# A gated network's first and last tiles in halves, and split weights whose rests are made by adding transfers

## The chip, the cores and the metric

The kernel runs as one program on one core of a Trainium2 chip. The metric is the device time of a run in microseconds (us). The kernel before has a median of 1264.14 us over 3 runs (1260.24 to 1267.88). One further execution was recorded by the hardware profiler; rows of that record are what this document quotes. Engines are named as the profile names them: PE is TensorE (PEld its weight loads), DVE is VectorE, ACT is ScalarE, POOL is GpSimd, SP is SyncE, whose queue starts most transfers. "L257" is line 257 of the kernel before.

## The reference, cut to what matters

The program is a decoder trunk of two layers on x of 512 tokens by 1024 features, fp32. Layer 0 mixes tokens with a state-space block, layer 1 with a forgetting attention (FoX). Behind each mixer stands a gated network:

```python
def conv_ffn(h, w_up, conv_w, conv_b, w_down):
    up = h @ w_up                       # 1024 -> 2 * 2816
    a, b = jnp.split(up, 2, axis=-1)
    ap = jnp.pad(a, ((0, 0), (CONV_W - 1, 0), (0, 0)))
    a_conv = conv_b
    for i in range(CONV_W):             # CONV_W = 3, causal, per feature
        a_conv = a_conv + ap[:, i:i + S] * conv_w[i]
    return (jax.nn.silu(a_conv) * b) @ w_down   # 2816 -> 1024
```

Ahead of every block x is normalised by its root mean square and modulated by shift and scale; the block's result is gated and added to x. At the end stands one more root-mean-square norm. The change is in the second gated network, which is the last block, and in that final norm.

## The kernel before, in words

**Layout.** Features lie on the partitions, tokens along the free axis: h is 8 tiles of 128 features by 512 tokens. The two halves of 256 tokens are HALVES; work is cut by them wherever a norm is in the way, because a norm needs all features of a token, not all tokens. The 2816 inner features are 22 pairs f of tiles (m = 2f goes through the convolution and silu, m = 2f + 1 multiplies it).

**Split products.** PE multiplies at reduced precision, so every operand is cut into a high part and a rest: hi is the value rounded by a copy on ScalarE (L240), lo is value − hi, a subtraction on VectorE (L241). Both are in `put_parts` (L238). A product is then three matmuls: hi·hi, hi·lo, lo·hi (`mms`, L249; its matmul is L257). A weight tile is loaded by SP into a buffer named raw (L161; ring of three), and split into w_hi and w_lo (rings of five). The raw buffer is free for the next load when both parts are made. Activations are kept as a_hi and a_lo, written by the norm (L390 makes nm_h, L393 a_hi, L394 a_lo).

**`product` (L262).** It multiplies output tiles ms one after the other. With head = n, the first n tiles are made half by half, so that PE can begin when only the first 256 tokens are normed. With tail = n the last n tiles are made half by half, all for the first half and then all for the second, so that the norm of the first half runs beside the second half's products. The first half's factors are spread to rows by four small matmuls (`rms_rows`, L370) placed ahead of the very last tile's second half; the inverse roots come from a chain of eleven small VectorE instructions (`inv_root`, L351 to L361, rs_v to rs_y).

**Second gated network (`ffn`, L513, with `plain` = 0 to 3).** The pairs f = 0 to 3 (tiles m0 to m7) are plain split products; m0 and m1 are in halves (head 2). From f = 4 on `quarters` (L466) makes a pair by a scheme with 7 instead of 8 block products, of 12 matmuls with 256 columns each (L500): the weights a (a11, a12) and b (a21, a22) are used as they are and in sums s1 to s4 made by VectorE (L472), the activations in x sums (L442, a_hi + a_lo) and four forms (L449), which `forms_x` (L432) yields step by step, so that they can be made between the tiles of f = 0 to 3. The results of block products are copied by ScalarE (L507, nm_h) and added by VectorE. Weights are split four times for a quarter: a, (s1, s2), (s4, s3), a22.

The 22 pairs stand in four groups of 6, 5, 6 and 5. While group q is made, the down product of group q − 1 is made too, one or two of its 8 tiles behind every pair; the last group's down product follows at the end, its last 2 tiles in halves. Its evacuation (L323) adds to h and squares it for the final norm.

**Final norm (`norm_out`, L400).** For the first half ScalarE scales h into hg, VectorE multiplies it by the rows (L411), SP stores it (L413, four stores). For the second half PE turns the tiles first (L419), and then ScalarE and VectorE apply rs_y (L424, L425, into o_tok), so that the chain of inv_root runs beside the turning. hg of the first half and o_tok share the room of a_lo, hg of the second half has that of a_hi.

**Order.** The order on each engine is fixed when the program is built, by a scheduler that works from the order of the code, priorities (`issue_after`, `behind`) and its own estimates; on the chip each engine then takes its instructions strictly in that order and waits by semaphores.

Of the kernel before, what the change touches and what calls it, by code (L numbers as in the profile page):

```python
# [8 lines left out]
F32 = mybir.dt.float32  # L9
F32R = mybir.dt.float32r  # L10
I32 = mybir.dt.int32
AF = mybir.ActivationFunctionType
# [26 lines left out]

GROUPS = (11, 11)  # L40
QGROUPS = (6, 5, 6, 5)
FIRST = (("c", (KT,)), ("s5_prm", (3, G // 2)), ("s5_eye", (64,)), ("s5_causal", (L,)))
REST = (
    ("ident", (P,)), ("ada_b", (4, 24)), ("norm_g", (4, KT)), ("final_g", (KT,)), ("cmask", (P,)), ("fox_bf", (NH,)),
# [10 lines left out]
class Trunk:  # L55
# [6 lines left out]
    def __init__(self, tc, io, ctx):  # L62
        self.tc, self.nc, self.io, self.ctx = tc, tc.nc, io, ctx
        nc = self.nc
        pool = lambda name, bufs, **k: ctx.enter_context(tc.tile_pool(name=name, bufs=bufs, **k))
        self.const = pool("const", 1)
        self.act = pool("act", 1)
        self.wpool = pool("wpool", 3)
        self.tmp = pool("tmp", 2)
        self.small = pool("small", 2)  # L70
        self.dram = pool("dram", 1, space=DRAM)
        self.mm = pool("mm", 4, space=PSUM)
        self.aux = pool("aux", 4, space=PSUM)
        self.bg = []
        self.acc = None
        self.pending = None

        self.first = self.load_pack("first", FIRST)
        self.c = self.first["c"]
        self.ones = self.const.tile([P, P], F32, name="ones")  # L80
        nc.vector.memset(self.ones, 1.0)
        self.sc = self.const.tile([P, KT], F32, name="sc")
        nc.scalar.activation(self.sc, self.c, AF.Silu)
        self.sc32 = self.const.tile([P, KT, 32], F32, name="sc32")

        self.sel = self.const.tile([P, 6], F32, name="sel")
        nc.gpsimd.memset(self.sel, 0.0)
        for q in range(4):
            for c in (q, 4 + q % 2):
                nc.gpsimd.memset(self.sel[32 * q:32 * q + 1, c:c + 1], 1.0)  # L90
        self.par = [self.const.tile([P, 24], F32, name=f"par{i}") for i in range(4)]
        self.ga = [self.const.tile([P, KT], F32, name=f"ga{i}") for i in range(4)]
# [139 lines left out]
    def split(self, src, shape, pool=None, bufs=WB):  # L232

        hi, lo = ((pool or self.wpool).tile(shape, F32R, name=n, bufs=bufs) for n in ("w_hi", "w_lo"))
        self.put_parts(hi, lo, self.raw(shape, src))
        return hi, lo

    def put_parts(self, hi, lo, src):  # L238
        nc = self.nc
        nc.scalar.activation(hi, src, AF.Copy)  # L240
        nc.vector.tensor_tensor(lo, src, hi.bitcast(F32), ALU.subtract)  # L241

    def weights(self, w, nk, *pool):
# [17 lines left out]
    def product(self, w, ms, nk, x, evac, head=0, tail=0, after=None, ticks=0, halves=HALVES, tail_pool=(), first=None, step=None):  # L261


        ms = list(ms)
        full = slice(0, S)
        if head:
            wk = first or {m: self.weights(w[m], nk) for m in ms[:head]}
            ps = {m: self.mm.tile([P, S], F32, name="mmp") for m in ms[:head]}
            for c in halves:
                for k in range(nk):  # L270
                    for m in ms[:head]:
                        self.mms(ps[m][:, c], wk[m], x, k, nk, c)
                    self.finish_norm((k + 1) * head)
                    if step:
                        step(3)
            for m in ms[:head]:
                evac(m, ps[m], full)
                self.tick(ticks)
        for m in ms[head:len(ms) - tail]:
            wk = self.weights(w[m], nk)  # L280
            ps = self.mm.tile([P, S], F32, name="mmp")
            for k in range(nk):
                self.mms(ps, wk, x, k, nk, full)
                if step:
                    step()
            evac(m, ps, full)
            self.tick(ticks)
        if tail:
            last = ms[len(ms) - tail:]
            wk = {m: self.weights(w[m], nk, *tail_pool) for m in last}  # L290
            for c in HALVES:
                for m in last:
                    if c is HALVES[1] and m == last[-1]:
                        rb = self.rms_rows(y)
                    ps = self.mm.tile([P, S // 2], F32, name="mmp")
                    for k in range(nk):
                        self.mms(ps, wk[m], x, k, nk, c)
                    evac(m, ps, c)
                if c is HALVES[0]:
                    y = after[0](c)  # L300
                else:
                    y2 = after[0](c)
                    after[1](HALVES[0], y, rb)
            self.pending = lambda: after[1](HALVES[1], y2)
# [95 lines left out]
    def norm_out(self, out):  # L400

        nc = self.nc

        def apply(cols, y, rb=None):
            last = cols is HALVES[1]
            hg = self.act.tile([P, KT, S // 2], F32, name="hg", tag="a_hi" if last else "a_lo")
            if not last:
                for k in range(KT):
                    nc.scalar.activation(hg[:, k], self.h[:, k, cols], AF.Copy, scale=self.final_g[:, k:k + 1])
                for k in range(KT):  # L410
                    nc.vector.tensor_tensor(hg[:, k], hg[:, k], rb, ALU.mult)  # L411
                    if k % 2:
                        nc.sync.dma_start(out[0][:, k - 1:k + 1], hg[:, k - 1:k + 1])  # L413
                return
            turned = [[pl.tile([P, S], F32, name=n) for pl, n in ((self.mm, "mmp"), (self.aux, "aux"))] for _ in range(2)]
            for k in range(KT):
                nc.scalar.activation(hg[:, k], self.h[:, k, cols], AF.Copy, scale=self.final_g[:, k:k + 1])
                for b in range(2):
                    nc.tensor.transpose(  # L419
                        turned[b][k // 4][:, k % 4 * P:(k % 4 + 1) * P], hg[:, k, b * P:(b + 1) * P], self.ident  # L420
                    )
            o = self.act.tile([P, 2, 2, S], F32, name="o_tok", tag="a_lo")
            for b in range(2):
                nc.scalar.activation(o[:, b, 0], turned[b][0], AF.Copy, scale=y[:, b:b + 1])  # L424
                nc.vector.tensor_scalar(o[:, b, 1], turned[b][1], y[:, b:b + 1], None, op0=ALU.mult)  # L425
                for j in range(2):
                    (nc.scalar if j == 0 else nc.sync).dma_start(out[1][:, b, j], o[:, b, j])

        return (self.rms_stats, apply), None


    def forms_x(self, pool, x):  # L432

        nc = self.nc
        H, N = KT // 2, S // 2
        t1, t2 = HALVES
        b = []
        for j, n in enumerate(("ghi1", "glo1")):
            t = pool.tile([P, H, S], F32, name=f"x{j}", tag=n)
            for c in HALVES:  # L440
                k = slice(j * H, (j + 1) * H)
                nc.vector.tensor_tensor(t[:, :, c], x[0][:, k, c].bitcast(F32), x[1][:, k, c].bitcast(F32), ALU.add)  # L442
                yield
            b.append(t)
        self.tx = {}
# [18 lines left out]
    def quarters(self, pool, l, f, x, finish):  # L464
# [10 lines left out]
        def parts(src, names, *where):  # L475
            hi, lo = ((where[0] if where else self.wpool).tile(
                [P, len(names) * H, P], F32R, name=n, tag=(where[1] + n if where else n), bufs=1 if where else WB
            ) for n in ("w_hi", "w_lo"))
            self.put_parts(hi, lo, src)
            for j, n in enumerate(names):  # L480
                w[n] = hi[:, j * H:(j + 1) * H], lo[:, j * H:(j + 1) * H]

# [48 lines left out]
    def ffn(self, i, l, x, nxt, ticks=0, plain=None):  # L531

        nc, tc = self.nc, self.tc
        with tc.tile_pool(name=f"ffn{l}", bufs=1, reuse_waits="tile") as pool:
# [40 lines left out]
            for q, n in enumerate(groups):  # L575
# [4 lines left out]
                        down(q, range(KT))  # L580
                    continue
                for j, f in enumerate(fs):
                    if f in plain:
                        up([f], head=0 if f else 2)
                        if f == 0:
                            todo.append(self.forms_x(pool, x))
                        for _ in range(3):
                            if todo and next(todo[0], True):
                                todo.pop()
                    else:  # L590
                        while todo:
                            if next(todo[0], True):
                                todo.pop()
                        self.quarters(pool, l, f, x, gated)
                    if q:
                        down(q - 1, range(j * KT // n, (j + 1) * KT // n))
            down(last, range(KT), tail=2, tail_pool=(pool, 4))
        return y

    def dump(self, out):  # L600
# [920 lines left out]
```

## Time and profile before

| | before |
|---|---|
| median of 3 runs | 1264.14 us (1260.24 to 1267.88) |
| the profiled execution's own time | 1263.7 us |
| its span | 1261.9 us |
| PE busy | 1235.6 us, 98% of the span |
| DVE busy | 897.0 us, 71% |
| ACT busy | 566.6 us, 45% |
| POOL busy | 56.5 us, 4% |
| DMA | 183.21 MB, mean 145 GB/s |
| mean granted PE clock | 0.994 |
| second gated network | about 893 to 1250 us |

Times in rows are microseconds from the span's start. A row of a timeline has start, duration, engine, line, operation, output <- inputs, shapes, and in square brackets how long the engine stood idle ahead of it and what ended that. "x3" puts neighbouring instructions of one kind together; durations of matmuls overlap, since they are pipelined, so the pace of PE is read from the chain of work, where pieces of PE follow each other.

### The profile page before, as it was taken

The numbers are of one execution on the slowest core, as the hardware profiler recorded it, in microseconds if no ns is written. First come the engines' busy times: TensorE is split into PE (matmuls) and PEld (weight loads), VectorE is DVE, ScalarE is ACT, GpSimd is POOL, SyncE is SP. The second block draws the span as 40 slices with busy tenths as digits, with TensorE's granted clock in tenths as the row PEclk, the third lists the DMA queues.
The fourth block names the chain that finished last, engine by engine and source line by source line (L and its number), as shares of the span: only waits on it lengthen the run. The fifth ranks groups of instructions, "written<-read, shape, count | busy, mean of one in ns | idle before, by whom it ended". The sixth has DMA issues, their size and how long they took to land.

```text
span 1261.9 us, 19246 instructions
## 1 busy us (share of the span) xinstructions
PE 1235.6 (98%) x7410; PEld 1022.5 (81%) x7410; DVE 897.0 (71%) x1606; ACT 566.6 (45%) x1041; POOL 56.5 (4%) x103
## 2 busy tenths in 40 slices
PE   7999999999999999999999999999999999999996
PEld 2566678898878778788799888878879999999985
DVE  7978887578764646656566567766899878887854
ACT  3544445335332233333433466664366555555543
POOL 0000000000000000000000233430000000000000
PEclk9999999999999999999999999999999999999998
DMA  9768667327644736544413424322043232343221
GB/s 360 242 217 257 209 197 237 102 96 240 227 149 142 227 120 229 168 151 152 149 35 117 153 99 140 126 88 68 19 134 105 90 118 82 105 129 97 91 73 67
DMA packets 73066, 183.21 MB, mean 145 GB/s; under 512 B 23079, under 2 KB 25471, under 8 KB 71951
## 3 DMA queue, kind: packets, MB, share of 16 engines
q1 hardware_dynamic: 72687, 181.46, 44.6%
q8 instruction: 58, 0.95, 0.3%
q10 hardware_dynamic: 288, 0.52, 0.1%
q14 instruction: 33, 0.27, 0.1%
HBM read 175.04 MB, written 6.92 MB: 144 GB/s over the span
## 4 chain that ended last, share of the span: by engine, by line
PE 93%; DVE 3%; ACT 1%; DMA 1%; issue 0%; SPq 0%; DVEq 0%; ACTq 0%
PE mmp L257 56%; PE mmp L500 10%; PE mmp L1102 4%; PE aux L500 4%; PE mmp L1267 2%; PE aux L908 2%; PE mmp L1131 2%; PE aux L1409 2%; PE aux L1392 1%; PE mmp L180 1%; PE aux L997 1%; PE aux L989 1%; PE aux L1362 1%; PE mmp L1042 1%; PE aux L947 1%; PE mmp L1072 1%
## 5 line engine op out<-in xcount | busy, mean ns | idle before, releaser
L240 ACT ACTIVATE w_hi<-raw 128x1024 fp32r<-128x1024 f32 (+4 forms) x201 | 186.3, 930 | 270.1 <-PE mmp L257 220.2
L241 DVE TENSOR_TENSOR w_lo<-raw,w_hi 128x1024 fp32r<-128x1024 f32 (+4 forms) x201 | 215.5, 1074 | 90.4 <-ACT w_hi L240 86.4
L257 PE MATMUL mmp<-a_hi,w_hi 128*128 128x512 f32 (+1 forms) x616 | 233.8, 382 | 3.5 <-ACT a_hi L393 2.1
L257 PE MATMUL mmp<-a_lo,w_hi 128*128 128x512 f32 (+1 forms) x616 | 231.2, 376 | 0.9 <-DVE a_lo L394 0.9
L257 PE MATMUL mmp<-a_hi,w_lo 128*128 128x512 f32 (+1 forms) x616 | 231.3, 377 | 0.0
L257 PE MATMUL mmp<-ghi,w_hi 128*128 128x512 f32 (+1 forms) x384 | 145.5, 379 | 0.0
L257 PE MATMUL mmp<-glo,w_hi 128*128 128x512 f32 (+1 forms) x384 | 145.0, 378 | 0.0
L257 PE MATMUL mmp<-ghi,w_lo 128*128 128x512 f32 (+1 forms) x384 | 145.0, 378 | 0.0
L257 PEld LDWEIGHTS mmp<-a_hi,w_hi 128*128 128x128 f32 x616 | 115.2, 188 | 28.1 <-ACT w_hi L240 3.3
L257 PEld LDWEIGHTS mmp<-a_hi,w_lo 128*128 128x128 f32 x616 | 115.8, 188 | 21.5 <-DVE w_lo L241 0.4
L257 PEld LDWEIGHTS mmp<-a_lo,w_hi 128*128 128x128 f32 x616 | 116.0, 188 | 20.9 <-DVE a_lo L394 1.3
L323 DVE SCALAR_TENSOR_TENSOR h<-mmp,par,h 128x512 f32<-128x512 f32 (+1 forms) x72 | 49.4, 689 | 65.3 <-PE mmp L257 65.1
L257 PEld LDWEIGHTS mmp<-ghi,w_lo 128*128 128x128 f32 x384 | 72.5, 189 | 14.6
L257 PEld LDWEIGHTS mmp<-ghi,w_hi 128*128 128x128 f32 x384 | 72.6, 189 | 14.0
L257 PEld LDWEIGHTS mmp<-glo,w_hi 128*128 128x128 f32 x384 | 72.5, 189 | 13.9
L208 DVE SCALAR_TENSOR_TENSOR ada_acc<-ada_raw,sc,ada_acc 128x1024 f32<-128x1024 f32 x49 | 62.8, 1281 | 29.1 <-DMA ada_raw<-in_ada_w 28.6
L500 PE MATMUL mmp<-w_hi 128*128 128x256 f32 x216 | 60.6, 280 | 0.0
L500 PE MATMUL mmp<-w_hi,w_lo 128*128 128x256 f32 x216 | 60.5, 280 | 0.0
L500 PE MATMUL mmp<-w_lo,w_hi 128*128 128x256 f32 x216 | 60.5, 280 | 0.0
L552 ACT ACTIVATE conv<-conv 128x512 f32<-128x512 f32 x44 | 27.7, 631 | 65.3 <-DVE conv L549 65.0
L1102 PE MATMUL mmp<-a_x,raw 128*128 128x512 f32 x112 | 56.5, 644 | 0.0
L241 DVE TENSOR_TENSOR w_lo<-sums,w_hi 128x1024 fp32r<-128x1024 f32 x36 | 43.8, 1220 | 4.8 <-ACT w_hi L240 4.7
(298 smaller groups left out, 2480.6 us busy)
## 6 DMA issues: line engine op xcount, KB each, us to landing
raw<-in_w_up SPq DMA_DIRECT2D x88, 512.0 KB, 3.8
ada_raw<-in_ada_w SPq DMA_DIRECT2D x56, 512.0 KB, 4.4
raw<-in_ada_w SPq DMA_DIRECT2D x40, 512.0 KB, 6.4
raw<-in_w_down SPq DMA_DIRECT2D x32, 384.0 KB, 3.1
raw<-in_w_down SPq DMA_DIRECT2D x32, 320.0 KB, 2.9
nf<-nfd SPq DMA_DIRECT2D x8, 1152.0 KB, 5.7
raw<-in_fox_qk SPq DMA_DIRECT2D x16, 512.0 KB, 3.6
h<-in_x SPq DMA_DIRECT2D x8, 512.0 KB, 5.5
```

The lines of the kernel that those rows point to most:

```text
L208: nc.vector.scalar_tensor_tensor(acc, w, self.sc[:, k:k + 1], acc, op0=ALU.mult, op1=ALU.add)
L240: nc.scalar.activation(hi, src, AF.Copy)
L241: nc.vector.tensor_tensor(lo, src, hi.bitcast(F32), ALU.subtract)
L257: self.last_mm = self.nc.tensor.matmul(o, wt, xt[:, cols], start=(k == 0 and n == 0), stop=(k == nk - 1 and n == 2),)
L323: self.nc.vector.scalar_tensor_tensor(self.h[:, m, cols], ps, self.par[i][:, 16 + m:17 + m], self.h[:, m, cols], op0=ALU.mult, op1=ALU.add,)
L500: self.last_mm = nc.tensor.matmul(o, wt[:, k], xt[:, k], start=(first and k == 0 and n == 0), stop=(k == H - 1 and n == 2), skip_group_che ...
L552: nc.scalar.activation(t, t, AF.Silu)
L908: nc.tensor.matmul(ps[g2][:, j, cols], x[rows, a + j, r].rearrange("p c j -> p (c j)"), self.rr[rows, planes, q, :], start=(j == 0 and r = ...
L1102: nc.tensor.matmul(ps, w[m][:, k, :], x[:, k], start=(k == 0), stop=(k == KT - 1))
L1131: nc.tensor.matmul(gps[m], wt, xt[:, k], start=(k == 0 and part == 0 and xt is yhi), stop=(k == KT - 1 and part == 1))
L1267: self.last_mm = nc.tensor.matmul(ps[q, b][:, :n], xt[:, k, tb], wt, start=(k == 0 and i == 0), stop=(k == KT - 1 and i == 2),)
L1409: nc.tensor.matmul(pv[:, c * P:], self.v[:, hp, k, r].rearrange("p t d -> p (t d)"), pp[:, r, c + 3 * k:NB + 3 * k, :].rearrange("p b t -> ...
```

## The change

1. m0, m1 and m2 are made in halves (head 3 over the first two pairs), m3 in full behind them. The forms are stepped four at a time instead of three.
2. The x sums of the forms are issued after the last a_lo of the norm.
3. The last network's last four down tiles are in halves instead of two; `rms_rows` of the first half stands ahead of the third of these four tiles in the second half.
4. Both halves of hg lie in one tile in a_hi's room; o_tok alone uses a_lo's.
5. `put_parts` can make the rest in another way. ScalarE copies the value a second time with sign −1 into lo, where it is rounded as hi is, and a transfer of GpSimd's queue adds raw to it, so that lo is value − hi again. It is used for a, for a22, and for the down tiles made beside pairs of groups 1 to 3 (60 splits); the sums s1 to s4, the plain tiles and the last down product keep the subtraction. Raw is free when the transfer has landed.

```diff
...
 GROUPS = (11, 11)
 QGROUPS = (6, 5, 6, 5)
+TAIL = 4
...
         self.aux = pool("aux", 4, space=PSUM)
         self.bg = []
         self.acc = None
+        self.adds = False
         self.pending = None
         self.first = self.load_pack("first", FIRST)
...
     def split(self, src, shape, pool=None, bufs=WB):
         hi, lo = ((pool or self.wpool).tile(shape, F32R, name=n, bufs=bufs) for n in ("w_hi", "w_lo"))
-        self.put_parts(hi, lo, self.raw(shape, src))
+        self.put_parts(hi, lo, self.raw(shape, src), self.adds)
         return hi, lo
-    def put_parts(self, hi, lo, src):
+    def put_parts(self, hi, lo, src, adds=False):
+
         nc = self.nc
         nc.scalar.activation(hi, src, AF.Copy)
+        if adds:
+            nc.scalar.activation(lo, src, AF.Copy, scale=-1.0)
+            nc.gpsimd.dma_start(lo, src, accum_op=ALU.add)
+            return
         nc.vector.tensor_tensor(lo, src, hi.bitcast(F32), ALU.subtract)
     def weights(self, w, nk, *pool):
...
             wk = {m: self.weights(w[m], nk, *tail_pool) for m in last}
             for c in HALVES:
                 for m in last:
-                    if c is HALVES[1] and m == last[-1]:
+                    if c is HALVES[1] and m == last[tail // 2]:
                         rb = self.rms_rows(y)
                     ps = self.mm.tile([P, S // 2], F32, name="mmp")
                     for k in range(nk):
...
     def norm_out(self, out):
         nc = self.nc
+        rooms = []
         def apply(cols, y, rb=None):
             last = cols is HALVES[1]
-            hg = self.act.tile([P, KT, S // 2], F32, name="hg", tag="a_hi" if last else "a_lo")
+            if not last:
+                rooms.append(self.act.tile([P, 2, KT, S // 2], F32, name="hg", tag="a_hi"))
+            hg = rooms[0][:, int(last)]
             if not last:
                 for k in range(KT):
                     nc.scalar.activation(hg[:, k], self.h[:, k, cols], AF.Copy, scale=self.final_g[:, k:k + 1])
...
         nc = self.nc
         H, N = KT // 2, S // 2
         t1, t2 = HALVES
+        normed = self.last_lo.ins
         b = []
         for j, n in enumerate(("ghi1", "glo1")):
             t = pool.tile([P, H, S], F32, name=f"x{j}", tag=n)
             for c in HALVES:
                 k = slice(j * H, (j + 1) * H)
-                nc.vector.tensor_tensor(t[:, :, c], x[0][:, k, c].bitcast(F32), x[1][:, k, c].bitcast(F32), ALU.add)
+                with self.tc.issue_after(normed):
+                    nc.vector.tensor_tensor(t[:, :, c], x[0][:, k, c].bitcast(F32), x[1][:, k, c].bitcast(F32), ALU.add)
                 yield
             b.append(t)
         self.tx = {}
...
             hi, lo = ((where[0] if where else self.wpool).tile(
                 [P, len(names) * H, P], F32R, name=n, tag=(where[1] + n if where else n), bufs=1 if where else WB
             ) for n in ("w_hi", "w_lo"))
-            self.put_parts(hi, lo, src)
+            self.put_parts(hi, lo, src, "s1" not in names and "s4" not in names)
             for j, n in enumerate(names):
                 w[n] = hi[:, j * H:(j + 1) * H], lo[:, j * H:(j + 1) * H]
...
                         down(q, range(KT))
                     continue
                 for j, f in enumerate(fs):
-                    if f in plain:
-                        up([f], head=0 if f else 2)
-                        if f == 0:
-                            todo.append(self.forms_x(pool, x))
-                        for _ in range(3):
+                    if f == 0:
+                        up([0, 1], head=3)
+                        todo.append(self.forms_x(pool, x))
+                    elif f in plain:
+                        if f > 1:
+                            up([f])
+                        for _ in range(4):
                             if todo and next(todo[0], True):
                                 todo.pop()
                     else:
...
                                 todo.pop()
                         self.quarters(pool, l, f, x, gated)
                     if q:
+                        self.adds = True
                         down(q - 1, range(j * KT // n, (j + 1) * KT // n))
-            down(last, range(KT), tail=2, tail_pool=(pool, 4))
+                        self.adds = False
+            down(last, range(KT), tail=TAIL if plain else 2, tail_pool=(pool, 4))
         return y
     def dump(self, out):
```

## The prediction

> **What bounds the kernel now.** First the page's head, then a table of busy time by stretch (start:end, length, then busy us and instructions of PE, PEld, DVE, ACT, POOL; granted clock; DMA share; GB/s) over the second gated network and the end: head, quarters, last products, output.
>
> ```profile
> span 1261.9 us, 19246 instructions
> 893.00:944.00 51.00, 47.44 (x255) 39.95 (x254) 47.85 (x79) 27.77 (x40) 0.00 (x0) 1.00 0.29 94
> 944.00:1210.00 266.00, 266.00 (x1884) 248.92 (x1884) 219.85 (x326) 140.91 (x218) 0.00 (x0) 1.00 0.33 102
> 1210.00:1240.00 30.00, 30.00 (x133) 24.21 (x132) 15.08 (x23) 12.52 (x23) 0.00 (x0) 1.00 0.12 35
> 1240.00:1262.00 22.00, 11.34 (x95) 10.69 (x93) 10.76 (x40) 5.97 (x13) 0.00 (x0) 0.82 0.27 96
> ```
>
> TensorE is busy without a gap from 944 to 1240. Only the head (3.6 us without it) and the output (10.7 us) have time to win. VectorE is at 83% of the quarters and nothing on PE waits for it, so relief there is worth nothing by itself. GpSimd is empty.
>
> The timeline of PE in the head (the bracket is idle time ahead and what ended it) and the chain of work that ended last:
>
> ```profile
> 903.74 0.97 PE L257 MATMUL mmp<-a_hi,w_hi 128*128 128x256 f32 x4 [1.30 <-ACT a_hi L393]
> 921.23 0.50 PE L257 MATMUL mmp<-a_hi,w_hi 128*128 128x512 f32 x1 [0.54 <-ACT w_hi L240]
> 922.18 21.81 PE mmp L257 x94
> 943.99 2.84 PE mmp L500 x24
> 1074.29 2.86 PE mmp L500 x24
> 1210.26 29.53 PE mmp L257 x126
> ```
>
> A matmul of 256 columns costs 2.86/24 = .119 us, one of 512 columns .232 (21.81/94) to .234 (29.53/126). A quarter, 84 of them, costs 10.0.
>
> **The change part by part.**
>
> **Head: m0 to m2 in halves instead of m0 and m1.** VectorE issues the norm's second half right behind rs_y in both versions, and rs_y has as much ahead of it, so I let PE meet the second half at 904.0, as now. By then three tiles have their first half instead of two. What is left then: 72 matmuls of 256 columns, 8.6 us, to 912.6, and 119 of 512 columns (five tiles; one matmul less by the overlap of the pipeline), 27.6, to 940.2. Against 943.99 that is −3.8: the half tile moved ahead (2.9), and .75 of waits for w_hi.
>
> It costs a new wait. The forms are now stepped four at a time, and the built order of VectorE has the multiply of tiles m4 and m5 (it waits until PE ends m5), then form 3, its rest, then m6's rest. ScalarE has form 3's w_hi ahead of m6's w_hi. So m6 cannot start until this chain has run behind m5's end:
>
> ```profile
> 918.27 0.69 DVE L556 TENSOR_TENSOR conv<-conv,mmp 128x512 f32<-128x512 f32 x1 [0.41 <-ACT conv L552]
> 925.57 1.22 DVE L449 TENSOR_TENSOR raw<-x,x 128x1024 f32<-128x1024 f32 x1
> 926.84 2.36 DVE L241 TENSOR_TENSOR w_lo<-raw,w_hi 128x1024 fp32r<-128x1024 f32 x2
> 929.20 1.06 ACT L240 ACTIVATE w_hi<-raw 128x1024 fp32r<-128x1024 f32 x1 [0.20 <-DMA raw<-in_w_up]
> ```
>
> .1 + .6 (multiply) + 1.15 (form 3) + 1.06 + 1.06 (two w_hi) = 4.0 to m6's first matmul; its third needs w_lo, behind form 3's: .1 + .6 + 1.15 + 1.06 + 1.15 + 1.15 = 5.2, less two matmuls done, so 4.9 in all. Quarters then start at 945.1: **+1.1**. Bounds: −3.8 if the wait is hidden, +2.5 if the norm's pace (.8 us of VectorE per k) holds the second half. The x sums, kept back until the last a_lo, only change places with it and stay inside this cover.
>
> **Rests by adding transfers.** In 60 splits (a11/a12, a22, and the down tiles done beside quarters) the subtraction goes; ScalarE gets a second copy (sign −1) and GpSimd's queue an add of raw into it: 18 of 512 KB, 18 of 256, 16 of 384, 8 of 320. Beside the quarters such splits cost (min/median/max ns, by shapes):
>
> ```profile
> L241 DVE TENSOR_TENSOR w_lo<-raw,w_hi x59: 678/947/1226, 950.7 to 1206.7; 128x512 fp32r<-128x512 f32 x17, 128x1024 fp32r<-128x1024 f32 x16, 128x768 fp32r<-128x768 f32 x16, 128x640 fp32r<-128x640 f32 x10
> L240 ACT ACTIVATE w_hi<-raw x59: 615/845/1065, 949.6 to 1205.9; 128x512 fp32r<-128x512 f32 x17, 128x1024 fp32r<-128x1024 f32 x16, 128x768 fp32r<-128x768 f32 x16, 128x640 fp32r<-128x640 f32 x10
> ```
>
> The 60 subtracts, 60 × .947 = 57 us of VectorE, lie beside PE: gain 0. ScalarE gets 60 × .845 = 51 us more, 141 of 266 to about 192, also beside PE. What matters: a raw buffer is free only once the add has landed, and SP's loads already wait for buffers (waits of SP's queue from 930 to 1210: us, times, longest; then issues of loads there and of stores at the end: KB, us to landing):
>
> ```profile
> SPq L161 <- DVE w_lo L241: 188.3, 51, 8.5
> raw<-in_w_up SPq DMA_DIRECT2D x30, 512.0 KB, 3.7
> raw<-in_w_down SPq DMA_DIRECT2D x16, 384.0 KB, 3.4
> raw<-in_w_down SPq DMA_DIRECT2D x13, 320.0 KB, 2.9
> out_dram<-hg SPq DMA_DIRECT2D x4, 256.0 KB, 2.5
> ```
>
> No add is in this trace. The nearest rows are these transfers: 2.5 for 256 KB, 3.7 for 512. An add reads its target too, and shares the engines with loads. I take about 5 for 512 KB and 4 for 256 KB, which are the plain ones plus a third to a half. The ends: 0 above the plain ones, and twice them or more.
>
> The first quarter. f4's a is loaded once form 3's rest leaves its buffer (m5's end, 71 matmuls of .232 behind 912.6, 929.0, and 4.1), 3.7, then hi and minus copy, 2.1: 938.9. Its add lands at 938.9 + X. Only then f5's b loads (3.7), is summed (three sums of .65), made into w_hi (1.06), and ScalarE has that ahead of f4's first copy of a product (.4). With .9 for hand-overs: 946.9 + X, against 945.1 + 36 × .119 = 949.4, when PE wants that copy. With X = 5 PE waits **2.5**; f6, with the same pattern behind a down tile, .5 by the same reckoning.
>
> The steady quarters, on f12 (ScalarE's copies of products, VectorE's sums; the chain of work):
>
> ```profile
> 1070.11 1.32 ACT L240 ACTIVATE w_hi<-raw 128x512 fp32r<-128x512 f32 x2
> 1078.28 1.29 DVE L472 TENSOR_TENSOR sums<-raw 128x512 f32<-128x512 f32 x2 [2.12 <-DMA raw<-in_w_up]
> 1080.04 0.39 ACT L507 ACTIVATE nm_h<-mmp 128x256 f32<-128x256 f32 x1 [0.47 <-PE mmp L500]
> 1080.54 1.06 ACT L240 ACTIVATE w_hi<-sums 128x1024 fp32r<-128x1024 f32 x1
> 1082.85 1.41 PE mmp L500 x12
> ```
>
> After the change f13's w_hi of sums stands ahead of that copy (c2), not behind it. a22's two copies end at 1071.4 as now; add X, load 3.6, two sums 1.3, w_hi 1.06, copy .4: 1077.8 + X, with .2 of hand-over 1078.0 + X. PE wants it at 1082.85. So the break-even is **X = 4.9 for 256 KB**; beyond it each us costs a us in each of some 15 quarters. At 4 nothing is lost; I add .2 for single late ones. Quarters: **+3.2**, bounds +.5 (X as plain) to +35 (X = 7).
>
> A price from elsewhere: the Trainium skill, "DMA: Bandwidth & Descriptors", section "Anatomy of one DMA — SWDGE (gpsimd) path", fits a GpSimd transfer as 2.0 us plus bytes over 436e3. An estimate by it is 3.2 us for 512 KB and 2.6 for 256, so f4 would wait .7 and the quarters cost about .7 in place of 3.2, the time 1263.5 in place of 1266; it is for copies, and no run here shows an add.
>
> **Last tiles: four in halves, one room for both halves of hg.** The end of the last product and VectorE behind it, DMA issues, and a chain of inv_root with nothing between:
>
> ```profile
> 1248.02 0.27 PE L419 MATMUL mmp<-rest,hg 128*128 128x128 f32 x1
> 1250.19 0.16 DVE L351 TENSOR_SCALAR rs_v<-aux 128x2 f32<-128x2 f32 x1 [0.42 <-PE aux L340]
> 1250.27 0.41 DVE L411 TENSOR_TENSOR hg<-hg,aux 128x256 f32<-128x256 f32 x1
> 1252.27 0.41 DVE L411 TENSOR_TENSOR hg<-hg,aux 128x256 f32<-128x256 f32 x1
> 1253.38 0.16 DVE L361 TENSOR_TENSOR rs_y<-rs_y,rs_t 128x2 f32<-128x2 f32 x1
> 1255.39 1.41 DVE L425 TENSOR_SCALAR o_tok<-aux,rs_y 128x512 f32<-128x512 f32 x2 [1.85 <-DMA out_dram<-hg]
> 887.53 0.16 DVE L351 TENSOR_SCALAR rs_v<-aux 128x2 f32<-128x2 f32 x1 [1.36 <-PE aux L340]
> 889.50 0.16 DVE L361 TENSOR_TENSOR rs_y<-rs_y,rs_t 128x2 f32<-128x2 f32 x1
> ```
>
> Six multiplies of hg stand inside the chain: 3.35 us against 2.13 without. Then o_tok waits 1.85 for the first half's output, whose buffer it takes. With rows of the first half two tiles earlier and both halves in one tile, the multiplies go ahead of the last product's end, and o_tok's buffer is free: −1.2 and −1.85, −3.1. Two more tiles in halves cost 2 × (30 × .119 − 15 × .234) = .1; PE may wait for the first half's rs_y at the earlier place, .4: **−2.5**, bounds −3.3 to 0 (if o_tok still waits for an output).
>
> **Sum.** +1.1 + 3.2 − 2.5 = +1.8 on the profiled run's 1263.7 (1.8 around its span): 1265.5. The median of 1264.14 lies .4 higher, so 1266. What a measurement here can tell from no change is .5%, 6.3 us: below 1257.8 or above 1270.5.
>
> **The rivals.**
> *Slow adds (slower).* One mechanism: a22's add holds its raw buffer past X = 4.9. For it: SP's loads waited 188 us for these buffers, and the adds put 60 more transfers beside 59 loads. Against: the plain rows are at 2.5, and DMA is at 33%. At X = 6.5 it is 1.6 × 15 = 24, at f4 and f6 some 4 more: about 1291; at 5.5 already 1276. A rule that would lengthen them: the Trainium skill, "SBUF — State Buffer", section "SBUF: two separate sides", has VectorE's two-port modes lock GpSimd out of writing descriptors; no row here shows it.
>
> *The head's wait hidden, adds quick (faster).* If m6's weights do not wait behind form 3, the head is −3.8, and with the quarters at +.5 and the tail at −3.1 the sum is −6.4: 1257.7, just over the bound. Against: the built order is fixed.
>
> *The tail doesn't do what it says.* o_tok waits for another output, or the earlier rows stall PE: tail 0, 1268.5, no change.
>
> **How the numbers follow.** My sum .38, all adds between 3 and 5.5 us, 1262 to 1270; slow adds .37; faster .17; idle tail .08. Faster .17, no change .44 (.38 and most of .08), slower .39. The likeliest gives 1266. Eight in ten: from 1258, the faster case, to 1290, slow adds at 6.5.
>
> **What would show it.** Head: PE idle of 4 to 5 us before m6, ended by ScalarE's w_hi, then w_lo; first quarter at 945. Adds: issues on GpSimd's queue with 4 to 5 us to landing, and PE waiting 2.5 in f4 for a copy behind w_hi. Quarters: 266 us long plus at most 3.5; more, with PE idle in every quarter, is the slow rival. Tail: no hg multiply behind rs_v, no DMA wait at o_tok, 7.2 us from the last product to o_tok becoming about 4.5. The prediction falls if adds take over 5 us for 256 KB, or if m6 has no wait.

## The result, and the profile after

The changed kernel takes 1283.55 us (median of 4 runs, 1281.65 to 1285.07) against 1263.47 us for the kernel before beside it: a ratio of 1.014, 95% interval 1.0118 to 1.0162. It is slower by 1.4%. The likeliest time of the forecast, 1266, did not come; the measured one lies inside its range, among the times that it gave to the rival of slow adds (1276 to 1291).

The profiled execution has a span of 1283.3 us against 1261.9. The timeline of PE gives the borders of the three stretches in both kernels: first product of the network, first block product, last block product (start, duration, engine, line). For the kernel before:

```profile
893.28 0.36 PE L257 MATMUL mmp<-a_hi,w_hi 128*128 128x256 f32 x1
943.83 0.28 PE L500 MATMUL mmp<-a_hi,w_hi 128*128 128x256 f32 x1
1209.97 0.28 PE L500 MATMUL mmp<-w_hi,w_lo 128*128 128x256 f32 x1
```

For the changed kernel, where L264 and L512 are the same two lines:

```profile
895.15 0.36 PE L264 MATMUL mmp<-a_hi,w_hi 128*128 128x256 f32 x1
949.07 0.28 PE L512 MATMUL mmp<-a_hi,w_hi 128*128 128x256 f32 x1
1234.13 0.41 PE L512 MATMUL mmp<-w_hi,w_lo 128*128 128x256 f32 x1
```

Differences of these starts make the table; the tail is what is left to the span. The stretch ahead of the network is the same program in all kernels, and its end still moves from 890.6 to 896.4 between executions, so stretches are compared and not times of day.

| us | before | changed | difference | forecast |
|---|---|---|---|---|
| ahead of the network | 893.3 | 895.2 | +1.9 | 0 |
| head | 50.55 | 53.92 | +3.4 | +1.1 |
| quarters | 266.14 | 285.06 | +18.9 | +3.2 |
| tail | 51.93 | 49.17 | −2.8 | −2.5 |
| span | 1261.9 | 1283.3 | +21.4 | +1.8 |

**Quarters.** PE, which waited for nothing here before, now waits nine times, 13.9 us, always for ScalarE's copy of a product (L519); the timeline of PE, the first two and the last of these waits:

```profile
965.81 0.38 PE L512 MATMUL mmp<-w_hi 128*128 128x256 f32 x1 [2.39 <-ACT nm_h L519]
982.97 0.39 PE L512 MATMUL mmp<-w_hi 128*128 128x256 f32 x1 [2.69 <-ACT nm_h L519]
1231.62 0.58 PE L512 MATMUL mmp<-w_hi 128*128 128x256 f32 x1 [3.42 <-ACT nm_h L519]
```

The waits make 13.9 of the 18.9 us. Behind the last one PE's granted clock was .50 from 1231 to 1234, which makes 1.5 more; the other 3.5 us were not taken apart. No wait here is for a rest.

The waits of SP's queue (us, times, longest) and the issues of the up weights' loads and of the adding transfers from 944 on (KB each, us to landing) say what is behind it. What the loads mostly waited for before, VectorE's subtraction, has become the landing of an add:

```profile
SPq L163 <- DMA w_lo<-raw: 266.8, 60, 8.1
...
raw<-in_w_up SPq DMA_DIRECT2D x33, 512.0 KB, 3.6
w_lo<-raw POOLq DMA_DIRECT2D x17, 512.0 KB, 5.7
w_lo<-raw POOLq DMA_DIRECT2D x16, 384.0 KB, 4.4
w_lo<-raw POOLq DMA_DIRECT2D x17, 256.0 KB, 3.3
w_lo<-raw POOLq DMA_DIRECT2D x8, 320.0 KB, 4.2
```

From the longest wait the chain of work (start, us, what) leads back to an add of a down tile. Its landing frees the buffer for the load of the next down tile, and ScalarE has that tile's w_hi ahead of the copy that PE waits for:

```profile
1222.15 3.96 DMA w_lo<-raw
...
1226.19 4.28 DMA raw<-in_w_down
...
1230.56 0.74 ACT w_hi L243
1231.29 0.28 ACT nm_h L519
```

**Head.** The wait at m6 is there as forecast, 4.0 us for w_hi and .2 for w_lo. What the forecast lacked stands in the windows behind it: the granted clock (the number ahead of the DMA share) is .50 for 5 us and .78 for two more.

```profile
934.98 0.79 PE L264 MATMUL mmp<-a_hi,w_hi 128*128 128x512 f32 x1 [4.02 <-ACT w_hi L243]
936.43 0.80 PE L264 MATMUL mmp<-a_hi,w_lo 128*128 128x512 f32 x1 [0.23 <-DVE w_lo L248]
...
935.00:940.00 5.00, 4.77 (x10) 3.28 (x11) 2.51 (x3) 2.36 (x3) 0.00 (x0) 0.50 0.67 205
940.00:942.00 2.00, 2.00 (x8) 1.62 (x7) 1.31 (x3) 1.67 (x3) 1.02 (x1) 0.78 0.68 272
942.00:948.00 6.00, 6.00 (x28) 4.94 (x28) 5.05 (x6) 4.96 (x6) 1.38 (x2) 1.00 0.92 199
```

**Tail.** VectorE's timeline at the end. The multiplies of hg (L421) are all ahead of rs_v, the chain takes 1274.75 to 1276.89, and o_tok follows with no wait for a transfer:

```profile
1273.43 0.74 DVE L421 TENSOR_TENSOR hg<-hg,aux 128x256 f32<-128x256 f32 x2
1274.75 0.16 DVE L358 TENSOR_SCALAR rs_v<-aux 128x2 f32<-128x2 f32 x1 [0.58 <-PE aux L347]
...
1276.73 0.16 DVE L368 TENSOR_TENSOR rs_y<-rs_y,rs_t 128x2 f32<-128x2 f32 x1
1276.99 1.41 DVE L435 TENSOR_SCALAR o_tok<-aux,rs_y 128x512 f32<-128x512 f32 x2
```

### The profile page after: what moved, and what is told of

Read it like the earlier page. It is cut to its first block, busy times and chain, and to the rows that moved or that the text cites. A ratio compares the mean times of both kernels' runs of the same rounds, so it can differ in the third digit from the quotient of the medians.

```text
span 1283.3 us, 19531 instructions
## 1 busy us (share of the span) xinstructions
PE 1243.4 (97%) x7464; PEld 1030.4 (80%) x7464; DVE 849.1 (66%) x1550; ACT 600.7 (47%) x1103; POOL 108.1 (8%) x163
## 4 chain that ended last, share of the span: by engine, by line
PE 82%; DMA 6%; DVE 5%; issue 4%; ACT 2%; POOL 0%; SPq 0%; DVEq 0%; POOLq 0%; ACTq 0%
PE mmp L264 52%; PE mmp L512 4%; PE mmp L1118 4%; DMA raw<-in_w_up 3%; DMA w_lo<-raw 2%; PE mmp L1283 2%; PE aux L924 2%; PE mmp L1147 2%; PE aux L512 2%; PE aux L1425 2%; PE aux L1408 1%; PE mmp L182 1%; PE aux L1005 1%; PE aux L1013 1%; DVE sums L484 1%
## 5 line engine op out<-in xcount | busy, mean ns | idle before, releaser
L264 PE MATMUL mmp<-a_hi,w_hi 128*128 128x512 f32 (+1 forms) x624 | 237.1, 381 | 6.3 <-ACT w_hi L243 4.0
L264 PE MATMUL mmp<-a_hi,w_lo 128*128 128x512 f32 (+1 forms) x624 | 234.3, 376 | 0.2 <-DVE w_lo L248 0.2
L264 PE MATMUL mmp<-a_lo,w_hi 128*128 128x512 f32 (+1 forms) x624 | 233.6, 375 | 0.0
L248 DVE TENSOR_TENSOR w_lo<-raw,w_hi 128x1024 fp32r<-128x1024 f32 (+3 forms) x141 | 159.4, 1133 | 95.6 <-ACT w_hi L243 91.9
L264 PE MATMUL mmp<-ghi,w_hi 128*128 128x512 f32 (+1 forms) x394 | 147.3, 374 | 0.0
L264 PE MATMUL mmp<-glo,w_hi 128*128 128x512 f32 (+1 forms) x394 | 146.8, 373 | 0.0
L264 PE MATMUL mmp<-ghi,w_lo 128*128 128x512 f32 (+1 forms) x394 | 146.6, 372 | 0.0
L264 PEld LDWEIGHTS mmp<-a_hi,w_hi 128*128 128x128 f32 x624 | 117.8, 189 | 30.4 <-ACT w_hi L243 6.1
L264 PEld LDWEIGHTS mmp<-a_hi,w_lo 128*128 128x128 f32 x624 | 118.0, 189 | 22.0 <-DVE w_lo L248 1.0
L264 PEld LDWEIGHTS mmp<-a_lo,w_hi 128*128 128x128 f32 x624 | 118.2, 189 | 19.5
L264 PEld LDWEIGHTS mmp<-ghi,w_lo 128*128 128x128 f32 x394 | 74.4, 189 | 14.1
L264 PEld LDWEIGHTS mmp<-ghi,w_hi 128*128 128x128 f32 x394 | 74.6, 189 | 13.5
L264 PEld LDWEIGHTS mmp<-glo,w_hi 128*128 128x128 f32 x394 | 74.5, 189 | 13.4
L246 POOL DMA_DIRECT2D w_lo<-raw x60 | 51.7, 862 | 319.1 <-ACT w_lo L245 120.5
L512 PE MATMUL mmp<-w_hi 128*128 128x256 f32 x216 | 62.8, 291 | 14.1 <-ACT nm_h L519 13.9
L484 DVE TENSOR_TENSOR sums<-raw 128x512 f32<-128x512 f32 x36 | 23.5, 689 | 72.8 <-DMA raw<-in_w_up 72.8
L243 ACT ACTIVATE w_hi<-sums 128x1024 fp32r<-128x1024 f32 x36 | 37.4, 1054 | 54.6 <-DVE sums L484 52.9
L512 PE MATMUL mmp<-w_hi,w_lo 128*128 128x256 f32 x216 | 61.0, 282 | 0.0
L512 PE MATMUL mmp<-w_lo,w_hi 128*128 128x256 f32 x216 | 61.0, 282 | 0.0
```

What stands on the lines that cost most here:

```text
L246: nc.gpsimd.dma_start(lo, src, accum_op=ALU.add)
L264: self.last_mm = self.nc.tensor.matmul(o, wt, xt[:, cols], start=(k == 0 and n == 0), stop=(k == nk - 1 and n == 2),)
L484: sub = lambda o, u, v, op=ALU.subtract: nc.vector.tensor_tensor(o, u, v, op)
L512: self.last_mm = nc.tensor.matmul(o, wt[:, k], xt[:, k], start=(first and k == 0 and n == 0), stop=(k == H - 1 and n == 2), skip_group_che ...
```

## The experiments

Theory: a raw buffer held until an add has landed makes loads, sums and copies late (19 us); the head loses by m6's wait and the low clock behind it; the tail gains. Rivals: ScalarE's second copies, crowded transfers, rests that come late by themselves, or the new head putting the quarters out of step. Stretches are read as above.

### The three parts, one by one

The changed kernel without adds:

```diff
-        if adds:
+        if False:
```

> The changed kernel with VectorE's subtraction in all 60 splits again; head, rooms and tail as changed. In the changed kernel's trace the quarters (first block product to the last product) take 285.3 us, 19.0 more than before, and the transfers or what they bring hold up SP's loads 60 times. If the transfers (or the second copies that go with them) make all of this, the quarters come back to 266 to 267 us and the time to about 1263.5 + 5.2 (head) - 2.9 (tail) = 1265.8. If the new head's order is what puts the quarters out of step, the quarters stay above 275 us and the time above 1274.

Measured: ratio .9997 (.9985 to 1.001). Head 54.2, quarters 266.1, tail 49.6. The quarters are back to the tenth, so the new head does nothing to them. By its stretches it should be 1.3 us slower than the one profiled execution of the kernel before; the interval ends about there.

The kernel before with the adds alone (printed in part: the 60 splits that ask for adds are those of the changed kernel):

```diff
...
         nc.scalar.activation(hi, src, AF.Copy)
+        if adds:
+            nc.scalar.activation(lo, src, AF.Copy, scale=-1.0)
+            nc.gpsimd.dma_start(lo, src, accum_op=ALU.add)
+            return
...
```

> The kernel before with the 60 adding transfers alone (old head, old tail). If the transfers carry the loss by themselves, the quarters take 283 to 287 us and the time is 1263.5 + 17 to 20 = 1281 to 1284. If the loss needs the new head (f4 starting late, with its weights late), the quarters take under 275 us and the time is under 1273.

Measured: 1.0219 (1.0198 to 1.024), quarters 290.3, 24.2 more, PE waiting 19 times, 17.1 us. The adds do it alone. With the old head they cost more than expected; no run shows why.

The kernel before with the tail's parts alone (printed in part: the place of `rms_rows` is changed too):

```diff
...
-            hg = self.act.tile([P, KT, S // 2], F32, name="hg", tag="a_hi" if last else "a_lo")
+            if not last:
+                rooms.append(self.act.tile([P, 2, KT, S // 2], F32, name="hg", tag="a_hi"))
+            hg = rooms[0][:, int(last)]
...
-            down(last, range(KT), tail=2, tail_pool=(pool, 4))
+            down(last, range(KT), tail=4 if plain else 2, tail_pool=(pool, 4))
```

> The kernel before with four last tiles in halves and both halves of hg in one room, nothing else. From the last product's first-half work to the end the changed kernel took 48.8 us against 51.6. If that is the tail's own doing: about 1263.5 - 2.9 = 1260.6. If it only came out so because PE's granted clock was lower there (0.96 and 0.90 in the last windows), the gain is 3.5 to 4.5: 1259 to 1260. If four halves cost as much as the room gains, no change.

Measured: .9986 (.9967 to 1.0004), not clear of the noise by itself. Its trace has the tail at 49.1, and every kernel with the new tail but one has it between 49.1 and 49.6, every one with the old between 51.7 and 51.9. The one is the kernel with adds for down tiles alone, below, at 51.2: its tail begins at a granted clock of .50 behind a wait of 3.05 us, and its first 156 products took 31.11 us where they take 29.68.

The kernel before with the head alone (printed in part: the x sums are behind the last a_lo too):

```diff
...
-                        up([f], head=0 if f else 2)
+                        up([0, 1], head=3)
...
-                        for _ in range(3):
+                        for _ in range(4):
```

> The kernel before with the new head alone (three tiles in halves, forms four at a time, x sums behind the last a_lo). The first quarter started 5.2 us later in the changed kernel: 4.0 + 0.2 of wait at m6, some 2.1 of matmuls at a granted clock of 0.50 behind it. If both belong to the head: 1263.5 + 5 = 1268.5, PE idle 4 us ahead of m6 and a clock of 0.5 for 4 to 6 us behind it. If the late start is taken up by the quarters (nothing in them waits for VectorE in the kernel before), less than 2 us remain: below 1265.5.

Measured: 1.0019 (1.0006 to 1.0032), some 2.4 us slower, less than expected. Head 52.9, with the same 4.02 us at m6, but the 46 matmuls behind it took 11.8 us where they took 12.8 in the changed kernel. By the windows' clocks it was at .50 for about 3.4 us here (.68 and .98 over 5 us each) and for about 6.8 us there. The old head isn't free of it: in two of its three profiled executions its 1.3 us of wait at the second half was followed by a clock of .5 to .6, and it took 51.9 instead of 50.55. Against those two executions the new head of the changed kernel is 2.0 us longer, not 3.4.

### What in the adds

ScalarE's second copies kept, VectorE adding raw to them:

```diff
-            nc.gpsimd.dma_start(lo, src, accum_op=ALU.add)
+            nc.vector.tensor_tensor(lo, lo.bitcast(F32), src, ALU.add)
```

> The changed kernel, with ScalarE's 60 second copies kept, and VectorE adding raw to them in place of the transfers. Theory of the buffers (a raw buffer is held until the transfer has landed, so loads, sums and copies of products come late): no transfer, so quarters 266 to 267 us as without the adds (266.1), time about 1264 to 1265. Rival, ScalarE (51 us of second copies stand ahead of the copies of products): quarters stay at 275 us or more, time above 1273.

Measured: 1.0005 (.9985 to 1.0025), quarters 266.1. ScalarE's 51 us cost nothing.

The adds reading the weights from DRAM, so that raw is free after ScalarE's copies (printed in part):

```diff
...
-            nc.gpsimd.dma_start(lo, src, accum_op=ALU.add)
+            nc.gpsimd.dma_start(lo, adds, accum_op=ALU.add)   # adds: the weights in DRAM
```

> The changed kernel, with the adding transfers reading the weights from DRAM a second time instead of from raw: raw is free after ScalarE's two copies. The rests still land late, and more is moved over DRAM. Theory of the buffers: the loads no longer wait for the transfers, so the quarters fall from 285 to 266 to 270 us, time 1264 to 1268. Rival, late rests (PE or the order behind it waits for lo itself) or rival, crowding (transfers beside loads stretch them): quarters stay at 280 us or more, time above 1278.

Measured: 1.0011 (.9992 to 1.003), quarters 268.6. The adds are even slower, and PE hardly minds; issues, and the waits of PE from 944 on:

```profile
w_lo<-in_w_up POOLq DMA_DIRECT2D x17, 512.0 KB, 7.2
w_lo<-in_w_up POOLq DMA_DIRECT2D x17, 256.0 KB, 6.6
...
PE aux L513 <- DMA w_lo<-in_w_up: 1.3, 1, 1.3
PE mmp L513 <- ACT nm_h L520: 0.6, 1, 0.6
```

A rest that lands 7 us late costs 1.3 us once. The held buffer, not the late rest, makes the loss.

Plain copies in place of adds, every instruction in the same order. This version leaves out the addition, so lo is raw and not the rest:

```diff
-            nc.gpsimd.dma_start(lo, src, accum_op=ALU.add)
+            nc.gpsimd.dma_start(lo, src.bitcast(F32R))
```

> The changed kernel with all its instructions in the same order, but the 60 transfers copy raw over lo instead of adding to it; the output is not the reference's, since lo is then raw and not the rest. It prices the addition itself. The adds took 5.7 us for 512 KB, 4.4 for 384, 4.2 for 320, 3.4 for 256 from issue to landing. If the addition makes them slow, plain ones take 3.7, 3.2, 2.9 and 2.5 as other transfers did, and the quarters fall to 266 to 272 us (time 1264 to 1270). If the queue and the crowd make them slow, they stay within 0.3 us of the adds, and the quarters at 280 us or more.

Measured: .9994 (.997 to 1.0017), quarters 266.9. SP's queue, GpSimd's queue (packets, MB, share of 16 engines' time) and issues from 944 on:

```profile
SPq L163 <- DMA w_lo<-raw: 246.6, 60, 8.2
...
q0 software_dynamic: 8352, 22.29, 22.9%
...
raw<-in_w_up SPq DMA_DIRECT2D x31, 512.0 KB, 3.4
w_lo<-raw POOLq DMA_DIRECT2D x17, 512.0 KB, 3.8
w_lo<-raw POOLq DMA_DIRECT2D x16, 384.0 KB, 3.6
w_lo<-raw POOLq DMA_DIRECT2D x17, 256.0 KB, 2.3
w_lo<-raw POOLq DMA_DIRECT2D x8, 320.0 KB, 2.6
```

In the changed kernel the same queue has:

```profile
q0 software_dynamic: 8560, 22.74, 44.7%
```

So the addition itself doubles the time that the packets take, and adds .8 to 1.9 us to each landing. Held buffers with plain copies cost .7 us, with adds 18.9. SP's queue waits for the landings almost as long in both (246.6 and 266.8 us), so this total names who holds the buffers and not what that costs PE.

The order that is built for ScalarE and VectorE changes with such edits, and could have been a cause too. With plain copies it is the changed kernel's. With adds from DRAM 33 of the 36 w_hi of sums stand at the same place among ScalarE's copies of products, the other three one copy earlier. So the order is not what these two versions repaired.

Subtractions by VectorE, and 60 copies of the same sizes from w_hi to DRAM on GpSimd's queue:

```diff
-            nc.scalar.activation(lo, src, AF.Copy, scale=-1.0)
-            nc.gpsimd.dma_start(lo, src, accum_op=ALU.add)
-            return
+            nc.gpsimd.dma_start(scratch, hi)   # scratch: a tile in DRAM
```

> The changed kernel with VectorE's subtraction in all 60 splits, and 60 transfers of the same sizes from w_hi to a scratch place in DRAM on GpSimd's queue, for which nobody waits. Theory of the buffers: nothing is held, quarters 266 to 267 us, time about 1264. Rival, crowding: the loads' median to landing rises from 3.6 us to above 4, and the quarters to 272 us or more.

Measured: .9989 (.9969 to 1.0009), quarters 266.1; the loads of 512 KB still land after 3.5 us. Crowding by plain transfers costs nothing. Crowding by adds without the holding is in the kernel that reads DRAM: the loads of 512 KB took 5.1 us there, and the quarters 2.5 us more, 1.3 of it the wait for a rest. In the changed kernel the loads landed after 3.6 us at the median, against 3.4 with plain copies; single ones took longer (4.28 us in the chain above). Where loads of 5.1 us cost so little, these can't make much of 18.9.

### Which adds

Adds for the 24 down tiles alone, then for a and a22 alone:

```diff
-            self.put_parts(hi, lo, src, "s1" not in names and "s4" not in names)
+            self.put_parts(hi, lo, src)
```

> The changed kernel with adding transfers for the 24 down tiles alone (384 and 320 KB); a and a22 have VectorE's subtraction again. With all 60 the quarters took 285.1 us, without any 266.1. If the down tile's add is the one in the chain (its buffer is the next one that a load of b takes, as in the stretch at 1088 to 1098), 14 us or more of the 19 stay: quarters 280 or more, time above 1278. If every held buffer of the ring of three counts alike, the loss goes by the time held beyond the subtraction: 24 x (4.3 - 0.8) = 84 of 84 + 18 x (5.7 - 1.2) + 18 x (3.4 - 0.7) = 214, so 7 us: quarters 273. If the adds must come together to use up the slack, under 3: quarters below 269.

```diff
-                        self.adds = True
+                        self.adds = False
```

> The changed kernel with adding transfers for a and a22 alone (18 of 512 KB, 18 of 256 KB); the down tiles have VectorE's subtraction again. If the down tile's add is the one in the chain: under 5 us of the 19 stay, quarters below 271. If every held buffer counts alike: 130 of 214 of the loss, 11.5 us, quarters 278. If they must come together: quarters below 269. My reckoning in the prediction (a22's add, break-even at 4.9 us, measured 3.4) gives 0 to 3 us, in f4 to f6 alone.

Measured: down tiles alone 1.0145 (1.0104 to 1.0186), quarters 285.7; a and a22 alone 1.0033 (1.0017 to 1.0049), quarters 269.4. So the down tiles' adds alone make 19.6 us in the profiled execution, as many as all 60 together; the 36 others 3.3. With the down tiles' adds there were only two runs, 1278.76 and 1286.29 us, and the trace is of the longer one.

The parts don't add up. One reason stands in the traces. With the down tiles' adds alone PE waits 12.5 us in the quarters, with all 60 13.9; but behind four of the five waits its granted clock was lowered, which took some 6.6 us more, against 1.5 with all 60. Three of these stretches (the clock is the number ahead of the DMA share; .83 over 10 us is 1.7 us lost):

```profile
1040.00:1050.00 10.00, 7.06 (x42) 6.57 (x41) 7.42 (x13) 4.15 (x7) 0.00 (x0) 0.83 0.34 97
1090.00:1100.00 10.00, 7.39 (x43) 6.51 (x42) 7.70 (x13) 4.45 (x7) 0.00 (x0) 0.84 0.34 98
1140.00:1150.00 10.00, 7.39 (x36) 6.33 (x35) 9.36 (x15) 4.51 (x7) 0.00 (x0) 0.83 0.31 93
```

That a wait for one add gives the other slack could be another reason, and so could the built order (in this kernel 9 of the 36 w_hi of sums stand elsewhere among ScalarE's copies); no run shows either.

With a and a22 alone PE has one wait. The chain of work behind it starts with an add of 512 KB that took 7.21 us and held the buffer of the next load:

```profile
964.06 0.38 PE L512 MATMUL mmp<-w_hi 128*128 128x256 f32 x1 [2.89 <-ACT nm_h L519]
...
945.11 7.21 DMA w_lo<-raw
...
952.47 4.79 DMA raw<-in_w_up
```

With the down tiles alone the chain of work ahead of one of five waits reads (start, us, what):

```profile
1082.59 6.42 DMA w_lo<-raw
1089.00 0.02 SPq L163
1089.03 0.03 issue
1089.06 3.22 DMA raw<-in_w_up
...
1093.24 0.69 DVE sums L484
...
1094.02 1.06 ACT w_hi L243
1095.08 0.28 ACT nm_h L519
1095.36 0.04 issue
1095.40 0.62 PE mmp L512 x3
```

A down tile's add of 6.4 us holds the buffer that a load of up weights takes next; the sums, their w_hi, and the copy that stands behind it on ScalarE follow. PE waited 2.61 there, so this add's break-even was 6.42 − 2.61 = 3.8 us. The down tiles' adds took 4.4 to 5.6 at the median. Only five of the 24 are followed by a wait, so most places had more slack than this one.

### A version that beats both

New head and tail, no adds, forms three at a time as before, which puts both parts of m6's weights ahead of the multiply that waits for m5:

```diff
-                        for _ in range(4):
+                        for _ in range(3):
...
-        if adds:
+        if False:
```

> New head and tail without adding transfers, and the forms stepped three at a time as in the kernel before, so that m6's two parts are made ahead of the multiply that waits for m5's end and ahead of forms 4 and 3. If that order is what made PE wait 4.0 us at m6 and lowered its granted clock behind it, the head (first product to first quarter) falls from 53.9 to 47 to 48 us, with no clock of 0.5 in it; with the tail's 49.3 and quarters of 266.1 the time is 1263.9 - 3 - 2.6 = 1258.3 (1257 to 1260). If another wait takes its place (m7's weights or form 3 late in the first quarter), the head or the first quarter is 2 us or more longer, the time 1260.5 or more.

Measured: 1256.56 us, ratio .9947 (.9931 to .9963), faster than the kernel before by about 6.7 us. Head 46.5, quarters 266.3, tail 49.1. The head's chain of work has no wait between the norm's second half and the first block product:

```profile
902.01 0.52 ACT a_hi L400
902.53 0.04 issue
902.57 36.18 PE mmp L264 x192
938.75 1.43 PE mmp L512 x12
```

Against the 54.2 of the same kernel with four steps, 7.7 us go: 4.25 of wait, and the rest, 3.4, fits the low clock (6.8 us at .50).

## Why the prediction was right or wrong

**What bounds the kernel: right.** PE alone set the quarters' length; 57 us of VectorE taken away gave nothing (quarters 266.9 with plain copies), and 51 us more of ScalarE cost nothing (266.1).

**Head: the wait right, its size short.** Named at 4.0 us to w_hi and .9 more for w_lo (its own terms make .7); measured 4.02 and .23, with two slow matmuls between. The step that failed is "quarters then start at 945.1", which let m6 and m7 run at full pace. They ran at a clock of .50 at first: 46 matmuls in 12.80 us where .232 each makes 10.7: 2.1 us, nearly the whole miss of 2.3. The Trainium skill, "TensorE: Matmul & The Clock Gate", section "Part 1: The HAM clock gate (the "warmup" mystery)", states that an idle window of about 3.4 us halves PE's clock and that some 3.4 us of work restore it. The traces agree behind the longest waits (4.02 and 3.42 us) that the clock goes to .50; it stayed there for about 6.8 and 3.4 us. They differ behind shorter ones: with the down tiles' adds alone two waits of 2.61 us were followed by a low clock, with a and a22 alone one of 2.89 us was not, and in the old head 1.3 us of wait, with short ones ahead of it, was followed by .5 to .6 in two executions.

**Quarters: the step that failed is the steady break-even.** It reckoned a22's add as the one that a load waits for ("a22's add, X = 4.9 for 256 KB"). For those adds the reckoning held: measured 3.3 to 3.7 us at the median, below 4.9. A kernel with the adds of a and a22 alone loses 3.3 us in the quarters against the forecast 3.2, by one wait of 2.89 for a copy behind w_hi, forecast as 2.5. That this agrees so well is in part luck: the wait fell in f5, one quarter later than named, and behind an add of 512 KB that took 7.2 us where 5 was reckoned. The 24 adds of down tiles were priced at nothing: the text said that raw is held by every add, and then followed one buffer only. In a ring of three a load takes the buffer whose turn it is, and for b that was a down tile's in the stretch shown; its break-even was 3.8 us, where the down tiles' adds took 4.4 to 5.6 at the median. By difference this made 15.6 of the 18.9 us, and alone it made 19.6. The price of an add was guessed near (5 and 4 us for 512 and 256 KB, measured 5.7 and 3.3), though 4 is not "a third to a half" above the 2.5 of its row but 60%.

**The rival of slow adds came by another buffer.** Its result, 1276 to 1291, holds the measured 1283.55; its condition (256 KB above 4.9 us) did not come true. It was right that an add holds a raw buffer beyond a break-even, and wrong in which one, so that the range reaches to the result is in part luck.

**The price from elsewhere.** The estimate by the fit of the Trainium skill, "DMA: Bandwidth & Descriptors", section "Anatomy of one DMA — SWDGE (gpsimd) path", was 3.2 us for 512 KB and 2.6 for 256. The plain copies measured, 3.8 and 2.3, are near it, and the adds of 512 KB, 5.7, are far from it; the forecast was right not to sum by it.

**Tail: right.** −2.8 against −2.5: the multiplies left the chain, and o_tok's 1.85 us of wait went.

**The sum.** +1.1 + 3.2 − 2.5 became +3.4 + 18.9 − 2.8; 1.9 us lie ahead of the network, where nothing was changed.

## What to carry to other kernels

When a transfer replaces an engine's last use of a ring buffer, the buffer's holding time changes for every user of the ring: price the latest user ahead of each load, not the one that the change seems to be about. An adding transfer took twice the packet time of a copy here, so relief of an engine that nothing waits for is no reason to use one. Waits of PE of 2.6 us and more were mostly followed here by 3.4 to 6.8 us at half clock, which cost 1.5 to 3.4 us beside the wait, so a reordering that makes such a wait vanish can be worth more than the wait.

## What the runs showed of the hardware that I had not expected

- Adding transfers of 22.7 MB in all took 44.7% of the 16 engines' time, copies of 22.3 MB in the same order 22.9%.
- Adds from DRAM land after 6.6 to 7.2 us whatever their size from 256 to 512 KB; adds within SBUF took 3.3 to 5.7 by size in the changed kernel, but with the down tiles' adds alone 320 KB took 5.6 and 384 KB 4.4.
- 60 plain transfers of 256 to 512 KB from w_hi to DRAM beside the loads left the quarters at 266.1 us to the tenth.
- The old head's waits, four from .25 to 1.30 us within 7 us, were followed by a clock of .5 to .6 in two of three profiled executions, and not in the third. Nor did a wait's length decide it in the quarters: behind 2.61 us the clock fell, twice, and behind 2.89 us it did not.
